# A 4-mixer decoder trunk on one core: its recorder's account learns which large buffers are free, and lane stages wait for them

## The chip, the core and the metric

The kernel runs on one core of a Trainium2 chip. The metric is the device time of one execution in microseconds (us); three runs of the kernel before gave 3057.76, 3059.04 and 3060.28 us, median 3059.04 us.

## The reference

Two layers of a trunk over 1024 prompt tokens and 8 x 8 sample tokens (1088 in all), model width 1024, in float32:

```python
for l in range(DEPTH):                       # 2 layers
    h = rmsnorm(x, norm_w[l]).astype(dt)
    proj = h @ w_in[l]                       # 1024 x 10 000 columns, in 16 parts
    ...
    y_a = a_b * conv_out * jax.nn.silu(a_z)  # A: short convolution
    y_s, h_r, h_i = s5_ssm(s_u, ...)         # B: S5, 32 groups of 16 channels, 64 complex states
    o_c, S_c = gated_recurrence(q_c, k_c, v_c, logf_c, st_hg[l])   # C: 4 heads
    o_d, S_d = gated_recurrence(q_d, k_d, v_d, gk, st_gla[l])      # D: 4 heads
    p = jnp.einsum('blnw,nwd->blnd', branches, w_branch[l])
    gates = jax.nn.sigmoid(m_logit.reshape(bsz, L, N_BRANCH, D_MODEL))
    x = x + jnp.sum(gates * p, axis=2) @ w_out[l]
```

The outputs are the normed tokens and the final states of the four mixers.

## The kernel before

All work is written from one recording program, the class `Trunk`. The large matrix products (projections, branch and output products) are its **main stream**: units of TensorE matmuls into tiles `mm`, each matmul 272 columns wide, each operand split into a high and a low part (`whi`, `wlo` for weights, `xh`/`xl`, `hi`/`lo`, `xc` for the tokens). VectorE makes each `wlo` and adds product results into half tiles `spot`; ScalarE makes each `whi`.

Beside it four **lanes** hold Python generators: `aux`, `s5l` (the S5 mixer), `tabs`, `rec` (the recurrences of C and D). After every few main matmuls `pump` looks whether a lane's next stage may be written now, and if so writes all instructions of that stage, on all engines. Engines work off their own instructions in the order written, so what `pump` decides is the order within each engine, PE's above all. `pump` decides by an **account**, the class `Book`: for every engine the time at which it will be free, and for every tile when it is written (`wr`) and last read (`rd`), from a cost for each instruction. A stage's `yield` says from which time on its next part may be written, and how many large tiles it takes (`need`).

Large tiles share 38 **places** of one pool (`NBIG`), handed round as they come free: whoever writes into a place first must wait until its last reader is done. In the account before, a new tile has no history, so its first writer counts as free to begin whenever its engine was last free.

The S5 mixer of a layer is built in **four blocks** (`s5_tables`, then `s5_scan`) while the gate products run (`GATES`), in the windows from 350 to 750 us for layer 0 and from 1840 to 2250 us for layer 1. A block's table part goes: GpSimd writes `tm` and `et` (six instructions of 128 x 512) and some 16 small ones (`qp`, `qt`); VectorE writes `tm` again from `Ppow` and `s5pk`, then `gt`, twice; TensorE turns `et` into `sm` and ScalarE copies it to `E`; GpSimd clears `tm`, VectorE copies `s5b` into it, TensorE multiplies `tm` with `s5b` and `gt`; two rounds of DMAs through `ksc` bring the result into `apad`; then TensorE multiplies `E` with `apad`, and the scan follows on VectorE. The scan of a block ends with products of `gt` and `H`, after which their places come free and the next block's `et` and `gt` take them. Ahead of block 1, VectorE prepares `s5b` through `s5tmp` from two GpSimd DMAs.

```python
            for ln in self.lanes:
                if (ln.q and ln.ready <= self.now and self.bank(ln.nsm) <= self.now and self.fits(ln)
                        and self.nc.free["dve"] <= self.now + self.backlog):
                    self.stage(ln)
```

Of the kernel before, what the change touches and what calls it, by code (L numbers as in the profile page):

```python
# [26 lines left out]
NBIG = 38  # L27
# [17 lines left out]
WBUF = 5  # L45
KEEP = 5
SPARE5 = 6
LEAD = 0.7


TURNS = (-2, 5, 11)
# [8 lines left out]
SEM = 0.05  # L60
# [36 lines left out]
class Book:  # L97
    def __init__(self, nc):
        self.nc = nc
        self.free = dict.fromkeys(("pe", "act", "dve", "pool", "sp", "dma"), 0.0)  # L100
        self.wr, self.rd = {}, {}
        self.table = None
        for attr, key in (("tensor", "pe"), ("scalar", "act"), ("vector", "dve"), ("gpsimd", "pool"), ("sync", "sp")):
            setattr(self, attr, Meter(self, getattr(nc, attr), key))

    def enter(self, key, op, aps, func):
        out, ins = aps[0], aps[1:]
        n = 1
        for d in max((x.shape[1:] for x in aps), key=lambda d: math.prod(d)):
            n *= d  # L110
        free, us = self.free, 1e-3
        parts = [self.parts_of(x) for x in aps]
        wr = [max(self.wr.get(k, 0.0) for k in p) for p in parts]
        rd = [max(self.rd.get(k, 0.0) for k in p) for p in parts]
        start = max([free[key]] + [t + SEM for t in wr[1:]])

        if key == "pe":
            start = max(start, rd[0] + SEM)
        else:
            start = max(start, rd[0] + SEM, wr[0] + SEM if op != "dma_start" else 0.0)  # L120
        if op == "dma_start":
            free[key] = start + (0.75 if key == "pool" else 0.45)
            size = math.prod(out.shape) * 4.0
            free["dma"] = max(free["dma"], free[key]) + size / 350e3
            end = free["dma"] + 1.9
        else:
            if key == "pe":
                m = math.prod(aps[-1].shape[1:]) if op == "matmul" else 128
                c = (m / 2400 + 0.011 if aps[1].dtype == F32R else 2 * max(m / 1200 + 0.004, 0.109)
                     if op == "matmul" else 0.11)  # L130
            elif key == "act":
                c = 0.155 + n * 0.87 * us
                if func in TABLED and func != self.table:
                    self.table = func
                    c += 1.3
            elif key == "dve":
                c = 0.15 + n * 1.05 * us
            else:
                c = 0.4 if n < 128 else 0.15 + n * (2.4 if op.startswith("tensor_t") or op in ("tensor_mul", "tensor_add", "tensor_sub")
                               else 0.9) * us  # L140
            free[key] = end = start + c
        for p in parts[1:]:
            for k in p:
                self.rd[k] = max(self.rd.get(k, 0.0), end)
        for k in parts[0]:
            self.wr[k] = end
# [25 lines left out]
class Trunk:  # L172
    def __init__(self, ctx, tc, a, o):
        self.tc, self.nc, self.a, self.o = tc, Book(tc.nc), a, o
        ctx.enter_context(tc.manual_schedule())
        mk = lambda name, bufs, **k: ctx.enter_context(tc.tile_pool(name=name, bufs=bufs, **k))
        self.cp = mk("const", 1)
        self.dr = mk("dram", 1, space=DRAM)
        self.ps = mk("psum", 2, space=PSUM)
        self.wp = mk("weights", 3)  # L180
        self.sp = mk("small", 1)
        self.bp = mk("big", NBIG)
        self.n = 0
        self.lanes = []
        self.banks = []
        self.alive = set()
        self.keep = KEEP
        self.backlog = BACKLOG
        self.inside = None
        self.more = False  # L190
        self.u_done = 0
        self.defer = []
# [19 lines left out]

    def free(self, *aps):
        for x in aps:
            self.alive.discard(x.name)

    def fits(self, ln):
        if ln.when and not ln.when():
# [3 lines left out]
    def pump(self):  # L222
        again = True
        while again:
            again = False
            self.weights()
            for ln in self.lanes:
                if (ln.q and ln.ready <= self.now and self.bank(ln.nsm) <= self.now and self.fits(ln)
                        and self.nc.free["dve"] <= self.now + self.backlog):
                    self.stage(ln)  # L230
                    again = True
                    break
# [33 lines left out]
    def big(self, shape, dt=F32, name="b"):  # L266
        n = 1
        for s in shape[1:]:
            n *= s
        assert n <= T, shape  # L270
        if self.inside is None:
            self.make_room()
        t = self.bp.tile([128, T], dt, tag="big", name=self.nm(name))
        v = t[:shape[0], :n]
        self.alive.add(v.name)
        assert len(self.alive) <= NBIG, sorted(self.alive)
        if len(shape) == 2:
            return v
        names = "abcdef"[: len(shape) - 1]
        return v.rearrange(f"p ({' '.join(names)}) -> p {' '.join(names)}", **dict(zip(names, shape[1:])))  # L280
# [72 lines left out]
    def parts_by(self, j):  # L353
# [38 lines left out]
                src = a22  # L392
                drop = [e + 2]

        old = self.places[-WBUF:][0] if len(self.places) >= WBUF else ()
        yield 1, max([self.at(src[:])] + [nc.rd.get(x, 0.0) + SEM for x in old])
        hi = self.wp.tile([128, 4, 128], F32R, tag="whi", name=self.nm("whi"), bufs=WBUF)
        lo = self.wp.tile([128, 4, 128], F32R, tag="wlo", name=self.nm("wlo"), bufs=WBUF)
        self.places.append((hi[:].name, lo[:].name))
        h, lv, r = hi[:], lo[:], src[:]  # L400
        if perm in (1, 2):
            h, lv = (x.rearrange("q k (p g) -> q k g p", g=8) for x in (h, lv))
# [311 lines left out]
    def make_plan(self):  # L714
        self.plan, self.seq = [], []
        self.loaded, self.done, self.raws, self.ws, self.sums_ = set(), set(), {}, {}, {}
        self.nraw = self.di = self.wi = 0
        self.preps, self.places = [], []
        self.merging = False
        self.left = [0.0] * RAWS  # L720

# [411 lines left out]
    def recurrence(self, l, nh, q, f, k, v, vs, sz, y_dst, nw_col, s0, sp_out, ss_out, gate=None):  # L1133
# [4 lines left out]
        if gate is not None:  # L1138
            yield self.at(k, *v), 1, 3
            f = yield from gate  # L1140
# [3 lines left out]
        own = self.prod([(q, k, slice(0, 128))], T, cuts, heads)  # L1144
# [13 lines left out]
            Ah = [(A[:, hh, :], hs) for hh, hs in enumerate(heads)]  # L1158
            self.free(q)
        B = k  # L1160
        yield self.at(*own[1]), 0
        own, ready = self.parts(own, cuts, heads)
        yield ready, 1, 1

# [48 lines left out]
        for _ in adv:  # L1213
            pass
        self.free(f)
        yield self.at(*pair[1]), 0
        pair, ready = self.parts(pair, cuts, heads)
        yield ready, 1
        for hh, hs in enumerate(heads):
# [117 lines left out]
        for b in range(8):  # L1337
            c = slice(TP + 8 * b, TP + 8 * b + 8)
# [30 lines left out]
        for hh in range(nh):  # L1369
# [22 lines left out]
            for c in cuts:  # L1392
                nc.vector.tensor_mul(sq[:, c], o[:, c], o[:, c])
                nc.scalar.activation(hi[:, c], o[:, c], AF.Square)
            yield self.at(hi), 0
            _, ready = self.parts((sq, (hi, lo)), cuts, heads[:1] if nh == 1 else [slice(0, 128)])
            self.alive.add(sq.name)
            yield ready, 1
            for s, n in SP:
                p = self.sm()  # L1400
# [5 lines left out]
            if len(sz) <= hh:  # L1406
                yield 0.0, 0, 0, lambda: len(sz) > hh
            nc.scalar.activation(sq, sq, AF.Exp, scale=-0.5)
            yield self.at(sq), 0
            nc.vector.tensor_mul(o, o, sq)  # L1410
            nc.vector.scalar_tensor_tensor(o, o, self.cols[:, nw_col:nw_col + 1], sz[hh], op0=ALU.mult, op1=ALU.mult)
            yield self.at(o), 0
# [6 lines left out]
    def gla_gate(self, l, pr):  # L1419
        nc = self.nc  # L1420
        f = self.big([128, T], name="f")
        m = self.big([128, T], name="m")
        bc = self.cols[:, 60 + 2 * l + pr:61 + 2 * l + pr]
        if pr == 0:
            self.r = self.big([48, T], F32R, name="r")
            for t0 in range(0, 9, 4):
                yield self.at(self.low), 1
                p = self.sm()
                n = min(512, T - 128 * t0)
                for t in range(t0, min(t0 + 4, 9)):  # L1430
                    r = 128 if t < 8 else 64
                    nc.tensor.transpose(p[:48, 128 * (t - t0):128 * (t - t0) + r], self.low[:r, t, :].bitcast(F32),
                                        self.ident[:r, :r])
                nc.scalar.activation(self.r[:, 128 * t0:128 * t0 + n], p[:48, :n], AF.Copy)
            self.free(self.low)
        yield self.at(self.r, self.wgk), 1
        for s, n in SP:
            p = self.sm()
            nc.tensor.matmul(p[:, :n], self.wgk[:, 128 * pr:128 * pr + 128], self.r[:, s:s + n], start=True, stop=True)
            nc.scalar.activation(f[:, s:s + n], p[:, :n], AF.Abs, bias=bc)  # L1440
            nc.vector.tensor_scalar(m[:, s:s + n], p[:, :n], bc, 0.0, op0=ALU.add, op1=ALU.min)
            yield 0.0, 1
        nc.scalar.activation(f, f, AF.Exp, scale=-1.0)
        nc.scalar.activation(f, f, AF.Ln, bias=self.ones[:])
        yield self.at(f), 0
        nc.vector.tensor_sub(f, m, f)
        nc.scalar.activation(f, f, AF.Exp, scale=1.0 / 16.0)
        self.free(m)
        if pr == 1:
            self.free(self.r)  # L1450
        yield self.at(f), 1, 1
        return f
# [862 lines left out]
```

## Time and profile before

| | |
|---|---|
| runs, median (lowest to highest) | 3059.04 us (3057.76 to 3060.28) |
| profiled execution: its time / span of its instructions | 3063.25 us / 3061.3 us |
| mean granted TensorE clock | 0.984 of 2.4 GHz |
| TensorE matmuls busy | 2947.9 us (96%) |
| VectorE / ScalarE / GpSimd busy | 1931.8 / 1110.3 / 389.6 us (63 / 36 / 13%) |
| share of the chain that ended last | PE 81%, DVE 7%, issue 4%, ACT 3%, DMA 2% |

PE is TensorE's matmul row, DVE is VectorE, ACT ScalarE, POOL GpSimd, SPq the queue of DMA issues. All instructions carry line 88 (89 in the changed kernel), the recorder's call, so they are told apart by tiles. The granted clock of TensorE has two levels, 0.50 (1.2 GHz) and 1.00 (2.4 GHz). Span and time of the profiled execution differ by 1.95 us, the work around the first and last instruction.

### The profile page before, as it was taken

The page shows a single profiled execution, that of the slowest core. Times are in us where ns is not written, and L with a number is a line of the kernel's source. Part 1 is how long each engine was busy: PE and PEld are TensorE (multiplying, and loading weights), DVE is VectorE, ACT ScalarE, POOL GpSimd, SP SyncE. Part 2 cuts the span into 40 slices and gives each one's busy share as a digit, 9 for nine tenths or more (in the row PEclk, how much of TensorE's full clock was granted, in tenths as well). Part 3 has the DMA queues.
Part 4 walks back from the last instruction along what each step waited for, and adds up shares of the span by engine and source line. Part 5 has one row for each costly group of instructions (what it writes and reads, how often), then busy time and mean ns, then how long its engine had stood idle before and what let it go on. Part 6 is the DMA issues. An engine that isn't in the chain of part 4 may idle for free.

```text
span 3061.3 us, 55591 instructions
## 1 busy us (share of the span) xinstructions
PE 2947.9 (96%) x22890; PEld 2862.4 (94%) x22890; DVE 1931.8 (63%) x3396; ACT 1110.3 (36%) x1932; POOL 389.6 (13%) x432
## 2 busy tenths in 40 slices
PE   7999999999999999989999999999999999999998
PEld 6999899999999999989889999999899999999997
DVE  5776676775656466868455666777645565577662
ACT  5332433333333426243343243333333344344321
POOL 2000202220000020213010002211100000103120
PEclk9999999999999999999999999999999999999999
DMA  4422333334212115435233223333421221245332
GB/s 119 162 71 61 101 111 107 106 97 143 61 47 66 40 39 183 153 102 195 88 128 107 62 72 118 100 102 110 162 63 47 63 67 37 75 160 159 133 136 89
DMA packets 318609, 309.41 MB, mean 101 GB/s; under 512 B 18497, under 2 KB 269649, under 8 KB 318357
## 3 DMA queue, kind: packets, MB, share of 16 engines
q1 hardware_dynamic: 316516, 302.02, 31.3%
q0 software_dynamic: 1840, 3.86, 0.4%
q8 instruction: 180, 2.95, 0.4%
q14 instruction: 73, 0.59, 0.1%
HBM read 217.16 MB, written 88.65 MB: 100 GB/s over the span
## 4 chain that ended last, share of the span: by engine, by line
PE 81%; DVE 7%; issue 4%; ACT 3%; DMA 2%; POOL 1%; SPq 1%; DVEq 0%; POOLq 0%; ACTq 0%
PE mm L88 70%; PE sm L88 11%; DVE wlo L88 1%; SPq L88 1%; ACT whi L88 1%; DMA apad<-usc 1%; DVE att L88 1%; DVE spot L88 1%; POOL et L88 1%; POOL tm L88 0%; DVE yb L88 0%; ACT L88 0%; DMA s5b<-in_s_b_im_dram 0%; DVE gt L88 0%; DVE wsum L88 0%
## 5 line engine op out<-in xcount | busy, mean ns | idle before, releaser
L88 PE MATMUL mm<-xc,whi 128*128 128x272 f32 x3136 | 526.7, 290 | 8.9 <-DVE spot L88 7.9
L88 PEld LDWEIGHTS mm<-xc,whi 128*128 128x128 f32 x3136 | 445.4, 191 | 12.7 <-issue 5.8
L88 DVE TENSOR_TENSOR wlo<-wraw,whi 128x512 fp32r<-128x512 f32 x400 | 315.8, 792 | 215.4 <-ACT whi L88 214.4
L88 PE MATMUL mm<-hi,whi 128*128 128x272 f32 (+2 forms) x1928 | 410.9, 293 | 12.5 <-ACT hi L88 4.3
L88 PE MATMUL mm<-lo,whi 128*128 128x272 f32 (+2 forms) x1928 | 409.5, 292 | 4.8 <-DVE lo L88 4.8
L88 PE MATMUL mm<-hi,wlo 128*128 128x272 f32 (+2 forms) x1928 | 409.2, 292 | 0.4 <-DVE wlo L88 0.4
L88 PE MATMUL mm<-xh,whi 128*128 128x272 f32 (+1 forms) x1720 | 370.5, 295 | 9.1 <-ACT spot L88 3.4
L88 PE MATMUL mm<-xl,whi 128*128 128x272 f32 (+1 forms) x1720 | 367.3, 293 | 11.7 <-DVE xl L88 11.7
L88 PE MATMUL mm<-xh,wlo 128*128 128x272 f32 (+1 forms) x1720 | 367.8, 294 | 3.4 <-DVE wlo L88 3.4
L88 ACT ACTIVATE whi<-wraw 128x512 fp32r<-128x512 f32 x400 | 272.8, 686 | 155.9 <-PE mm L88 124.2
L88 PE MATMUL mm<-xc,wlo 128*128 128x272 f32 x1568 | 326.6, 290 | 0.0
L88 PEld LDWEIGHTS mm<-hi,whi 128*128 128x128 f32 x1928 | 306.8, 191 | 15.8 <-issue 5.2
L88 PEld LDWEIGHTS mm<-lo,whi 128*128 128x128 f32 x1928 | 306.5, 191 | 7.1 <-DVE lo L88 5.8
L88 PEld LDWEIGHTS mm<-hi,wlo 128*128 128x128 f32 x1928 | 306.0, 191 | 2.6 <-issue 1.2
L88 PEld LDWEIGHTS mm<-xl,whi 128*128 128x128 f32 x1720 | 274.4, 191 | 13.4 <-DVE xl L88 12.7
L88 PEld LDWEIGHTS mm<-xh,whi 128*128 128x128 f32 x1720 | 274.3, 191 | 12.4 <-ACT whi L88 3.9
L88 PEld LDWEIGHTS mm<-xh,wlo 128*128 128x128 f32 x1720 | 273.9, 191 | 6.5 <-DVE wlo L88 5.3
L88 PEld LDWEIGHTS mm<-xc,wlo 128*128 128x128 f32 x1568 | 247.6, 190 | 0.7 <-issue 0.7
L88 ACT ACTIVATE whi<-wsum 128x512 fp32r<-128x512 f32 x147 | 99.4, 677 | 205.3 <-DVE wsum L88 172.1
L88 DVE TENSOR_TENSOR spot<-spot,mm 128x544 f32<-128x544 f32 x181 | 129.6, 716 | 53.3 <-PE mm L88 50.7
L88 ACT ACTIVATE spot<-spot 128x544 f32<-128x544 f32 x87 | 57.4, 660 | 266.2 <-DVE spot L88 264.6
L88 DVE TENSOR_TENSOR wlo<-wsum,whi 128x512 fp32r<-128x512 f32 x147 | 114.1, 776 | 54.5 <-ACT whi L88 53.3
(367 smaller groups left out, 5162.9 us busy)
## 6 DMA issues: line engine op xcount, KB each, us to landing
wraw<-in_w_in_dram SPq DMA_DIRECT2D x328, 256.0 KB
g<-gsc SPq DMA_DIRECT2D x64, 544.0 KB
gsc<-spot SPq DMA_DIRECT2D x116, 272.0 KB
y<-ysc SPq DMA_DIRECT2D x24, 544.0 KB
wraw<-in_w_branch_dram SPq DMA_DIRECT2D x48, 256.0 KB
ysc<-o SPq DMA_DIRECT2D x16, 544.0 KB
wo<-in_w_out_dram SPq DMA_DIRECT2D x16, 512.0 KB
out_dram<-S SPq DMA_DIRECT2D x12, 512.0 KB
```

Of the source, the lines that this page charges most:

```text
L88: r = fn(*a, **kw)
```

## The change

Four things change in the recorder, none in the arithmetic. (1) The account keeps for each large tile the place that it takes: `gone` lists the tiles given back, the least recently used one is taken as predecessor, and the new tile inherits the time at which that one was last used. (2) `pump` writes a lane's stage only when the `need` places that it will take are free by the account (`places`). (3) Costs: a small GpSimd instruction 0.55 instead of 0.4, a DMA with rows under 64 elements eight times its bytes. (4) Five yields in the recurrences and the gate of D, reached 30 times a layer, become due 1.0 earlier (`AHEAD`): the VectorE instructions behind them are written before ScalarE, by the account, is done. `self.places` of the weights is only renamed `pairs_`.

```diff
+AHEAD = 1.0
...
+        self.turn += 1
+        for x in aps:
+            self.used[x.name] = self.turn
...
-            size = math.prod(out.shape) * 4.0
+            size = math.prod(out.shape) * 4.0 * (8 if out.shape[-1] < 64 else 1)
...
-                c = 0.4 if n < 128 else 0.15 + n * (2.4 if op.startswith("tensor_t") or op in ("tensor_mul", "tensor_add", "tensor_sub")
+                c = 0.55 if n < 128 else 0.15 + n * (2.4 if op.startswith("tensor_t") or op in ("tensor_mul", "tensor_add", "tensor_sub")
...
-            self.alive.discard(x.name)
+            if x.name in self.alive:
+                self.alive.discard(x.name)
+                self.gone.append(x.name)
+
+    def left_at(self, x):
+
+        return max(d.get(k, 0.0) for d in (self.nc.rd, self.nc.wr) for k in (x, x + "b")) + SEM
+
+    def places(self, n):
+
+        if not n:
+            return 0.0
+        return max([self.left_at(x) for x in sorted(self.gone, key=lambda x: self.nc.used.get(x, 0))[:n]])
...
+                        and self.places(ln.need) <= self.now
...
+        old = min(self.gone, key=lambda x: self.nc.used.get(x, 0))
+        self.gone.remove(old)
+        self.nc.rd[v.name] = self.nc.rd[v.name + "b"] = self.left_at(old)
+        self.nc.used[v.name] = self.nc.turn
...
-        yield self.at(*own[1]), 0
+        yield self.at(*own[1]) - AHEAD, 0
...
-            yield self.at(sq), 0
+            yield self.at(sq) - AHEAD, 0
```

Up to the start of S5 in layer 0 nothing moves. From there, in three places:

VectorE, layer 0, the start of block 2's tables, before: `tm_5291` and `gt_5290` are block 2's; the `fs` and `s5pk` rows are the last of block 1's scan.

```order
L88 TENSOR_TENSOR s5pk_3869<-fs_5222,f_617_5223 128x4x8 x2
L88 TENSOR_TENSOR spot_3390<-spot_3853,mm_5130 128x544
L88 TENSOR_TENSOR wlo_5212<-wsum_5143,whi_5211 128x512
L88 TENSOR_TENSOR wraw_5071<-wraw_4864,wraw_5071 128x512
L88 TENSOR_TENSOR wlo_5271<-wraw_5071,whi_5270 128x512
L88 TENSOR_TENSOR tm_5291<-Ppow,s5pk_3869 128x512 x2
L88 TENSOR_TENSOR gt_5290<-tm_5291 64x4x128 x2
L88 TENSOR_TENSOR wsum_5144<-wraw_5105,wsum_5144 128x512
```

The same place now (`tm_5366`, `gt_5365`):

```order
L89 TENSOR_TENSOR s5pk_3892<-fs_5320,f_626_5321 128x4x8 x2
L89 TENSOR_TENSOR wlo_5400<-wraw_5116,whi_5399 128x512
L89 TENSOR_TENSOR spot_3853<-spot_1560,mm_5333 128x544
L89 TENSOR_TENSOR wsum_5443<-wraw_5314,wraw_5395 128x512
L89 TENSOR_TENSOR wsum_5444<-wsum_5443,wraw_5116 128x512
L89 TENSOR_TENSOR spot_3853<-spot_3853,mm_5418 128x544
L89 TENSOR_TENSOR spot_3852<-spot_1560,mm_5333 128x544
L89 TENSOR_TENSOR wlo_5453<-wsum_5444,whi_5452 128x512
L89 TENSOR_TENSOR wlo_5466<-wraw_5397,whi_5465 128x512
L89 TENSOR_TENSOR wlo_5498<-wsum_5443,whi_5497 128x512
L89 TENSOR_TENSOR tm_5366<-Ppow,s5pk_3892 128x512 x2
```

Nine rows of the main stream now stand ahead of the first `tm` where four stood. On TensorE, from block 1's last `gt` row to block 2's first `tm` row, the order holds 186 main matmuls where it held 76; between GpSimd's `et` and VectorE's `tm` pass 66 to 86 main matmuls in every block of either layer (before: 74 in the first block, none in the other three). The last block's last rows stand 337 main matmuls later in layer 0 and 241 later in layer 1; the first products of layer 0's first recurrence 34 later, those of layer 1 at the old place, and the last recurrence ends at its old place in both layers.

VectorE, layer 0, ahead of block 1, before: the `s5tmp` and `s5b` rows read what the two GpSimd DMAs bring.

```order
L88 TENSOR_TENSOR s5tmp_3870<-s5b_3868,zfac 128x256 x2
L88 TENSOR_TENSOR s5b_3868<-s5tmp_3870 128x256
L88 TENSOR_TENSOR s5tmp_3870<-s5b_3868,zfac 128x256 x2
L88 TENSOR_TENSOR s5b_3868<-s5tmp_3870 128x256
L88 TENSOR_TENSOR wlo_4009<-wraw_3745,whi_4008 128x512
L88 TENSOR_TENSOR spot_1560<-spot_3852,mm_3987 128x544
```

And now:

```order
L89 TENSOR_TENSOR wsum_4039<-wsum_4038,wraw_3745 128x512
L89 TENSOR_TENSOR spot_1560<-spot_1560,mm_4009 128x544
L89 TENSOR_TENSOR s5tmp_3893<-s5b_3891,zfac 128x256 x2
L89 TENSOR_TENSOR s5b_3891<-s5tmp_3893 128x256
L89 TENSOR_TENSOR wlo_4056<-wsum_4039,whi_4055 128x512
L89 TENSOR_TENSOR wlo_4073<-wraw_3988,whi_4072 128x512
L89 TENSOR_TENSOR spot_3390<-spot_3852,mm_3975 128x544
L89 TENSOR_TENSOR s5tmp_3893<-s5b_3891,zfac 128x256 x2
```

The first of these rows now stands 54 main matmuls later, behind two more `spot` rows; the DMAs themselves are written 18 main matmuls later.

VectorE, layer 0, start of the merge, before: `y` is mixer A's output, split for the first branch products; the `o` rows close a recurrence.

```order
L88 TENSOR_TENSOR wlo_12642<-wraw_12302,whi_12641 128x512
L88 TENSOR_TENSOR lo_12697<-y_12615,hi_12696 128x1088
L88 TENSOR_TENSOR wlo_12701<-wraw_12424,whi_12700 128x512
L88 TENSOR_TENSOR o_12536<-o_12536,osq_12558 128x1088
L88 SCALAR_TENSOR_TENSOR o_12536<-o_12536,cols,sz_11530 128x1088
L88 TENSOR_TENSOR lo_12721<-y_12617,hi_12720 128x1088
```

And now:

```order
L89 TENSOR_TENSOR o_12529<-o_12529,osq_12550 128x1088
L89 SCALAR_TENSOR_TENSOR o_12529<-o_12529,cols,sz_11527 128x1088
L89 TENSOR_TENSOR wlo_12643<-wraw_12383,whi_12642 128x512
L89 TENSOR_TENSOR lo_12699<-y_12615,hi_12698 128x1088
L89 TENSOR_TENSOR wlo_12703<-wraw_12428,whi_12702 128x512
L89 TENSOR_TENSOR lo_12719<-y_12617,hi_12718 128x1088
```

The pair of `o` rows moved from between the first two `lo` rows to ahead of the `wlo` row before them. Ahead of mixer B's products (`xl`) another such pair of `o` rows moves 22 main matmuls earlier.

## Rows read from the trace of the kernel before

**Rows 1.** The page, busy time of each engine: us, share, instructions.

```profile
PE 2947.9 (96%) x22890; PEld 2862.4 (94%) x22890; DVE 1931.8 (63%) x3396; ACT 1110.3 (36%) x1932; POOL 389.6 (13%) x432
```

**Rows 2.** Busy time by windows: length, PE, PEld, DVE, ACT, POOL (instructions), PE clock, DMA.

```profile
250.00:300.00 50.00, 50.00 (x404) 50.00 (x403) 35.02 (x52) 15.29 (x24) 0.80 (x2) 1.00 0.25 69
...
450.00:500.00 50.00, 45.89 (x375) 45.26 (x374) 32.41 (x56) 15.32 (x29) 18.25 (x25) 0.93 0.32 96
```

**Rows 3.** Waits of PE: tile, who ended it: us in total, times, longest.

```profile
PE sm L88 <- DVE tm L88: 16.8, 4, 4.4
PE mm L88 <- DVE spot L88: 14.3, 6, 3.9
PE mm L88 <- DVE xl L88: 11.7, 4, 3.7
PE sm L88 <- ACT E L88: 6.4, 2, 3.2
...
PE sm L88 <- DMA apad<-usc: 5.3, 5, 1.9
...
PE mm L88 <- DVE lo L88: 4.8, 2, 2.4
...
PE sm L88 <- POOL et L88: 3.1, 2, 1.6
```

**Rows 4.** Timeline of DVE, layer 0, tables of block 2: start, us, [idle before].

```profile
479.33 1.29 DVE L88 TENSOR_TENSOR tm<-Ppow,s5pk 128x512 f32<-128x512 f32 x2 [5.46 <-POOL et L88]
...
484.78 0.71 DVE L88 TENSOR_TENSOR spot<-spot,mm 128x544 f32<-128x544 f32 x1
...
488.15 0.82 DVE L88 COPY tm<-s5b 64x64 f32<-64x64 f32 x4
```

**Rows 5.** Timeline of POOL, the same block.

```profile
474.48 1.29 POOL L88 TENSOR_TENSOR et<-tm 128x512 f32<-128x512 f32 x1 [5.35 <-issue]
...
478.01 1.29 POOL L88 TENSOR_TENSOR et<-tm 128x512 f32<-128x512 f32 x1
479.24 0.83 POOL L88 COPY qp<-Qpow 128x4 f32<-128x4 f32 x2
...
487.57 0.40 POOL L88 MEMSET tm<- 128x368 f32 x1
```

**Rows 6.** Timeline of PE, layer 0, waits at block 2 and at block 3.

```profile
488.69 0.62 PE L88 MATMUL sm<-s5b,tm 128*32 128x16 f32 x4 [4.04 <-DVE tm L88]
...
578.27 0.77 PE L88 MATMUL mm<-xc,whi 128*128 128x272 f32 x4 [2.37 <-DVE spot L88]
```

**Rows 7.** Timeline of DVE, layer 0, ahead of block 1.

```profile
365.14 0.42 DVE L88 TENSOR_TENSOR s5tmp<-s5b,zfac 128x256 f32<-128x256 f32 x1 [3.67 <-DMA s5b<-in_s_b_im_dram]
...
369.68 0.68 DVE L88 TENSOR_TENSOR wsum<-wraw,wraw 128x512 f32<-128x512 f32 x1
370.40 1.67 DVE L88 TENSOR_TENSOR wsum<-wsum,wraw 128x512 f32<-128x512 f32 x1
```

**Rows 8.** Timeline of POOL, the same stretch.

```profile
369.73 1.79 POOL L88 TENSOR_TENSOR et<-tm 128x512 f32<-128x512 f32 x1
```

**Rows 9.** Windows as in rows 2, the nine stretches of S5 at clock 0.50, and their sum.

```profile
1996.17:1999.58 3.41, 3.41 (x29) 2.91 (x26) 0.29 (x1) 1.54 (x4) 0.00 (x0) 0.50 0.50 151
...
sum 51.21, PE 42.22 PEld 39.47 DVE 29.69 ACT 16.96 POOL 9.22; mean PE 4.69 PEld 4.39 DVE 3.30 ACT 1.88 POOL 1.02
```

**Rows 10.** Windows as in rows 2, stretches of the merge at clock 0.50.

```profile
1183.80:1187.21 3.41, 3.41 (x16) 3.26 (x15) 3.02 (x5) 1.27 (x3) 0.00 (x0) 0.50 0.29 81
...
2695.90:2699.32 3.42, 3.42 (x16) 3.40 (x16) 3.04 (x5) 1.53 (x3) 0.00 (x0) 0.50 0.34 92
```

**Rows 11.** Timeline of DVE, layer 0, start of the merge.

```profile
1176.84 1.29 DVE L88 TENSOR_TENSOR lo<-y,hi 128x1088 fp32r<-128x1088 f32 x1 [4.67 <-ACT hi L88]
...
1178.65 1.29 DVE L88 TENSOR_TENSOR o<-o,osq 128x1088 f32<-128x1088 f32 x1
...
1181.24 3.69 DVE L88 TENSOR_TENSOR lo<-y,hi 128x1088 fp32r<-128x1088 f32 x3
```

More of the change, by code (lines that the diff above doesn't have):

```diff
@@ L101, in __init__ @@
         self.wr, self.rd = {}, {}
+        self.turn, self.used = 0, {}
         self.table = None
@@ L186, in __init__ @@
         self.alive = set()
+        self.gone = [f"none{i}" for i in range(NBIG)]
         self.keep = KEEP
@@ L393, in parts_by @@
                 drop = [e + 2]
-        old = self.places[-WBUF:][0] if len(self.places) >= WBUF else ()
+        old = self.pairs_[-WBUF:][0] if len(self.pairs_) >= WBUF else ()
         yield 1, max([self.at(src[:])] + [nc.rd.get(x, 0.0) + SEM for x in old])
@@ L398, in parts_by @@
         lo = self.wp.tile([128, 4, 128], F32R, tag="wlo", name=self.nm("wlo"), bufs=WBUF)
-        self.places.append((hi[:].name, lo[:].name))
+        self.pairs_.append((hi[:].name, lo[:].name))
         h, lv, r = hi[:], lo[:], src[:]
@@ L717, in make_plan @@
         self.nraw = self.di = self.wi = 0
-        self.preps, self.places = [], []
+        self.preps, self.pairs_ = [], []
         self.merging = False
@@ L1215, in recurrence @@
         self.free(f)
-        yield self.at(*pair[1]), 0
+        yield self.at(*pair[1]) - AHEAD, 0
         pair, ready = self.parts(pair, cuts, heads)
@@ L1394, in recurrence @@
                 nc.scalar.activation(hi[:, c], o[:, c], AF.Square)
-            yield self.at(hi), 0
+            yield self.at(hi) - AHEAD, 0
             _, ready = self.parts((sq, (hi, lo)), cuts, heads[:1] if nh == 1 else [slice(0, 128)])
             self.alive.add(sq.name)
+            self.gone.remove(sq.name)
             yield ready, 1
@@ L1444, in gla_gate @@
         nc.scalar.activation(f, f, AF.Ln, bias=self.ones[:])
-        yield self.at(f), 0
+        yield self.at(f) - AHEAD, 0
         nc.vector.tensor_sub(f, m, f)
```

## The prediction

> **What bounds the kernel now.** The page first: TensorE's matmuls are busy 2947.9 us, 96% of the span, VectorE only 63% [rows 1]. So the kernel is bound by TensorE, and a change that leaves every matmul as it is can win only what TensorE idles (3061.3 - 2947.9 = 113 us) and what it loses at the lower clock. The windows say where. In a stretch with no S5 work TensorE is busy 50.00 of 50 us and gets through 404 matmuls, 0.124 us each; in a stretch in which S5 tables are built it is busy 45.89, gets through 375, and its mean clock is 0.93 [rows 2]. The list of TensorE's waits then says for whom [rows 3]. Three entries are S5 tables alone: VectorE's `tm` 16.8 us in 4 waits, ScalarE's `E` 6.4 in 2, GpSimd's `et` 3.1 in 2. Of the six waits for `spot` (14.3 us) one stands at block 3, 2.37 us long [rows 6], with a twin in layer 1. Tables therefore cost 16.8 + 6.4 + 3.1 + 4.7 = 31.0 us, and the other four `spot` waits, 9.6 us, stand ahead of block 1.
>
> The timelines of one block show why. GpSimd's first `et` can begin only when block 1's last product with `gt` has freed its place: 474.48, after idling [rows 5]. The second ends at 479.30, and until then VectorE stands 5.46 us at `tm` [rows 4], with `wlo` and `spot` rows of the main stream written behind it: the `spot` row comes at 484.78. GpSimd goes on with 16 small instructions and clears `tm` only at 487.57 to 487.97; VectorE's copy follows at 488.15, and TensorE, which had got there long before, goes on at 488.69 after 4.04 us [rows 6]. The cause is the order: VectorE's `tm` was written at the very point of the main stream at which the places came free, since the account let GpSimd begin in the past.
>
> **What the clock adds.** Nine stretches of S5 show a granted clock of 0.50, the level of 1.2 GHz; each but one begins in or right behind one of these waits. TensorE is busy 42.22 us in them [rows 9]. Leaving out the one that begins at 1996.17 (3.41 us, behind a DMA), 38.8 us at half speed lose at most 19.4 us.
>
> **The change, part by part.** It adds and removes no arithmetic; what counts is where rows stand.
>
> *Tables.* From `et` to VectorE's `tm` now lie 66 to 86 main matmuls, 8.2 to 10.7 us, and the trace needs 479.33 - 474.48 = 4.85 us [rows 4, 5]: no wait, with 3.3 us to spare. From the freed place to the end of the clearing it needs 487.97 - 474.48 = 13.5 us; TensorE's `tm` row now stands 186 main matmuls (23 us) behind, where it stood 76 (9.4 us). All 31.0 us should go. Bounds: 0 and -31.0.
>
> *Ahead of block 1.* VectorE stood 3.67 us at `s5tmp` for a DMA [rows 7], with `spot` behind it. These rows now stand 54 main matmuls (6.7 us) later, the DMAs 18 (2.2 us) later: 4.5 us gained. That covers layer 0; layer 1, where the longest `spot` wait was 3.9 us [rows 3], I leave 1.6 us. So -8.0 of 9.6; bounds 0 and -9.6.
>
> *Clock.* With the waits gone most of the 19.4 us comes back. Part of these stretches is many small S5 matmuls that stay, so I take -15; bounds 0 and -19.4.
>
> *What is late next.* Behind the `tm` product comes the way through two DMAs to `apad`, and there TensorE already waits 5.3 us in five of eight blocks [rows 3]. The slow stretches lie just in this way and gave the DMAs time; of the 15 us some will be waited for here. I take +5; bounds 0 and +15.
>
> *GpSimd beside VectorE.* In blocks 2 to 4 VectorE stood idle while GpSimd wrote `tm` and `et`; now it does main work there. Ahead of block 1 this can be seen: a `wsum` row takes 1.67 us instead of 0.68 [rows 7] beside an `et` of 1.79 us [rows 8], which takes 1.29 alone [rows 5]. Six such GpSimd instructions a block can each hold one VectorE row: at most 6 x 0.99 = 5.9 us. VectorE is busy 35.02 of 50 us without S5 [rows 2], so 8.5 us hold 2.5 us of slack. With half of the meetings, 3.0 - 2.5 = 0.5 us a block stays, 4 us in eight; bounds 0 and 8 x 3.4 = 27. I take +4, since the two `wsum` rows side by side show one hit and one not.
>
> The Trainium skill speaks against this change here: the page SBUF — State Buffer, section "Who interferes with whom", says that a VectorE instruction with two SBUF inputs contends with a GpSimd instruction that reads SBUF, and that the later one is fully blocked until the first is finished. The stretched row agrees, being 0.99 us longer where an `et` alone takes 1.29. By the rule all six would block for 1.29 us, 7.7 - 2.5 = 5.2 us a block, 42 us instead of 4.
>
> *Merge.* The `o` pair (1181.24 - 1178.65 = 2.6 us) moves ahead of the first `lo`, into time in which VectorE idled 4.67 us [rows 11], so the two waits for `lo`, 4.8 us [rows 3], should go: -4.8, bounds 0 and -4.8. The waits for `xl` (11.7 us in 4) lose such a pair out of a full VectorE queue too: up to 2.6 us a layer, of which I take 2: -4, bounds 0 and -11.7. The slow stretches behind the `lo` waits [rows 10] are worth 6.83 / 2 = 3.4 us at most: -2.
>
> *`AHEAD`, costs, renaming: nothing.* VectorE may stand up to 1.0 us at 60 places for ScalarE. What hides it: a stand of 5.46 us cost TensorE 4.04 [rows 4, 6] and one of 4.67 us cost 2.4 [rows 11, 3], so the first 1.4 us or more are covered by finished weights and free PSUM. Without cover it is 60 x 1.0 us; bounds 0 and +60, and I take the lower end, since 1.0 is under both covers. SP's queue keeps its issues, some of them moved.
>
> **The sum.** -31.0 - 8.0 - 15 + 5 + 4 - 4.8 - 4 - 2 = -55.8 us. The profiled execution took 3063.25 us, 4.2 above the median of the runs; off that it is 3007.5, off the median 3003.2. I predict 3003.
>
> **The rivals.**
> - *GpSimd now slows VectorE.* For it: the stretched row. Against: VectorE's 30% idle. At the upper bound 27 us instead of 4, and the clock falls again in eight blocks, up to half of the 15 us given back: 3003 + 23 + 7.5 = 3034; it reaches from 3022 to 3046. By the page's rule in place of the row it would be 3003 + 38 = 3041 before the clock.
> - *Nothing moves.* The account's guess of the place could be wrong, and the waits only change their names: 3059. Against: the distances in the order hold whatever place is taken.
> - *Slower: the last block comes too late.* It ends 337 and 241 main matmuls later, 42 and 30 us, among the recurrences, which `begin(3)` drains before the last branch. If the delay came through to there in full, TensorE would idle 72 us: 3075. It makes the kernel slower when over 62 us of the 72 (the gain and 6 us) arrive. Against: by the order the last recurrence ends at its old place in both layers.
> - *All terms at their best:* -31.0 - 9.6 - 19.4 - 4.8 - 11.7 - 3.4 = -79.9, so 2979.
>
> **How the numbers follow.** Forecast (2985 to 3022) 0.62; GpSimd slows VectorE (3022 to 3046) 0.18; nothing moves 0.06; slower 0.06; better than 2985 0.08. The range 2985 to 3046 holds the first two, 0.80; the forecast's own is 2985 to 3022. A change of under 0.2% (6 us) can't be told from none in this kernel. Faster: 0.62 + 0.18 + 0.08 = 0.88. Of "nothing moves" 0.04 falls within 6 us and 0.02 beyond; slower 0.06 + 0.02 = 0.08.
>
> **What the changed kernel's profile would show.** Tables: TensorE's waits for `tm`, `E` and `et` gone, VectorE's for `et` too. Head: no `s5tmp` wait of over 1.5 us for the DMA. Clock: mean of 0.988 or more, and fewer than five stretches at 0.50 in S5. `apad` waits 5 to 15 us. Merge: no `lo` wait. I am wrong if `spot` or `wlo` waits appear beside GpSimd's tables, if `apad` takes over what the tables give back, or if TensorE idles before the last branch.

## The result, and the profile after

The changed kernel took 2993.86 us (median of four runs, 2990.29 to 2994.76) beside 3059.66 us for the kernel before: ratio 0.9781, 95% interval 0.9764 to 0.9798, 66 us faster. The forecast was 3003, in a range of 2985 to 3046. Its profiled execution spans 2992.0 us at a mean clock of 0.992, 69.3 us less than before.

The page of the changed kernel, busy time of each engine (answers to [rows 1]):

```profile
PE 2926.8 (98%) x22890; PEld 2845.6 (95%) x22890; DVE 1944.8 (65%) x3396; ACT 1111.8 (37%) x1932; POOL 382.1 (13%) x432
```

TensorE idles 2992.0 - 2926.8 = 65.2 us where it idled 113.4, so 48.2 us of the gain are waits. The other 21.1 us are TensorE's own busy time, for the same 22890 matmuls: that is clock. The windows show both in one row, the window from 450 to 500 us as in the second of [rows 2], and behind it the only stretch of S5 that is left at 0.50:

```profile
450.00:500.00 50.00, 50.00 (x430) 49.85 (x428) 35.56 (x59) 17.78 (x31) 15.56 (x25) 1.00 0.39 120
...
668.27:671.69 3.42, 3.38 (x15) 3.38 (x16) 0.00 (x0) 1.31 (x3) 1.26 (x7) 0.50 0.22 81
```

TensorE's waits in the changed kernel (answers to [rows 3]):

```profile
PE mm L89 <- DVE xl L89: 10.7, 4, 3.2
...
PE mm L89 <- ACT hi L89: 4.5, 2, 2.5
...
PE sm L89 <- DMA apad<-usc: 3.2, 7, 0.7
PE sm L89 <- ACT ys L89: 3.1, 2, 2.1
...
PE mm L89 <- DVE lo L89: 0.5, 2, 0.2
```

VectorE's `tm` and `spot`, ScalarE's `E` and GpSimd's `et` are no longer in the list. `xl` has hardly moved, `apad` fell, and `ys` is new.

VectorE in block 2 of layer 0 (answers to [rows 4]):

```profile
485.60 0.69 DVE L89 TENSOR_TENSOR wlo<-wsum,whi 128x512 fp32r<-128x512 f32 x1
486.21 1.28 DVE L89 TENSOR_TENSOR tm<-Ppow,s5pk 128x512 f32<-128x512 f32 x2
```

GpSimd there (answers to [rows 5]):

```profile
475.20 1.29 POOL L89 TENSOR_TENSOR et<-tm 128x512 f32<-128x512 f32 x1 [2.67 <-issue]
...
479.06 1.29 POOL L89 TENSOR_TENSOR et<-tm 128x512 f32<-128x512 f32 x1
...
496.09 0.41 POOL L89 MEMSET tm<- 128x368 f32 x1 [10.49 <-DVE gt L89]
```

The second `et` ends at 480.35 and `tm` begins at 486.21, straight behind a `wlo` row and with no wait in brackets: 5.9 us to spare. GpSimd still idles ahead of `et`; only nobody stands behind it now.

### The profile page after: what moved, and what is told of

Its sections match the earlier page's. It is cut to its first block, busy times and chain, and to the rows that moved or that the text cites. A ratio compares the mean times of both kernels' runs of the same rounds, so it can differ in the third digit from the quotient of the medians.

```text
span 2992.0 us, 55595 instructions
## 1 busy us (share of the span) xinstructions
PE 2926.8 (98%) x22890; PEld 2845.6 (95%) x22890; DVE 1944.8 (65%) x3396; ACT 1111.8 (37%) x1932; POOL 382.1 (13%) x432
## 4 chain that ended last, share of the span: by engine, by line
PE 86%; DVE 6%; DMA 3%; ACT 2%; issue 2%; SPq 1%; POOL 0%; DVEq 0%; POOLq 0%; ACTq 0%
PE mm L89 75%; PE sm L89 12%; SPq L89 1%; DMA apad<-usc 1%; DVE wlo L89 1%; DVE att L89 1%; DMA wraw<-in_w_branch_dram 1%; DVE yb L89 0%; ACT whi L89 0%; DVE mg L89 0%; DVE g L89 0%; DMA sz<-szs 0%; DVE o L89 0%; DVE xl L89 0%; DVE xf L89 0%
## 5 line engine op out<-in xcount | busy, mean ns | idle before, releaser
L89 PE MATMUL mm<-xc,whi 128*128 128x272 f32 x3136 | 519.4, 288 | 1.0 <-ACT xc L89 0.8
L89 PEld LDWEIGHTS mm<-xc,whi 128*128 128x128 f32 x3136 | 439.2, 188 | 2.4 <-ACT xc L89 1.0
L89 DVE TENSOR_TENSOR wlo<-wsum,whi 128x512 fp32r<-128x512 f32 x147 | 120.2, 818 | 55.2 <-ACT whi L89 53.2
```

The lines of the kernel that those rows point to most:

```text
L89: r = fn(*a, **kw)
```

## The experiments

Ratios are to the kernel before, measured beside each run; differences are ratio times 3060 us, since medians of different groups of runs differ by some 3 us.

| kernel | median us | ratio, 95% interval | us against before |
|---|---|---|---|
| changed kernel | 2993.9 | 0.9781 (0.9764 to 0.9798) | -67.0 |
| parts 1 and 2 | 3013.8 | 0.9843 (0.9829 to 0.9858) | -48.0 |
| part 1 | 3013.8 | 0.9842 (0.9829 to 0.9856) | -48.3 |
| clamp instead of part 1 | 3013.0 | 0.9846 (0.9832 to 0.9859) | -47.1 |
| all but the inheritance | 3038.8 | 0.9928 (0.9915 to 0.9940) | -22.0 |
| part 3 | 3049.8 | 0.9958 (0.9944 to 0.9971) | -12.9 |
| all but the DMA cost | 3003.8 | 0.9815 (0.9802 to 0.9829) | -56.6 |
| part 4 | 3046.9 | 0.9949 (0.9937 to 0.9962) | -15.6 |
| all but AHEAD | 3000.2 | 0.9805 (0.9792 to 0.9819) | -59.7 |
| changed, `et` twice | 2998.7 | 0.9789 (0.9772 to 0.9806) | -64.6 |
| changed, tables on VectorE | 2990.2 | 0.9765 (0.9749 to 0.9781) | -71.9 |
| changed, YLAG 1 | 2987.1 | 0.9749 (0.9734 to 0.9764) | -76.8 |
| the same, products with sz last | 2986.9 | 0.9751 (0.9736 to 0.9767) | -76.2 |

**Parts 1 and 2, and part 1 alone.** From the changed kernel:

```diff
-AHEAD = 1.0
+AHEAD = 0.0
-            size = math.prod(out.shape) * 4.0 * (8 if out.shape[-1] < 64 else 1)
+            size = math.prod(out.shape) * 4.0
-                c = 0.55 if n < 128 else ...
+                c = 0.4 if n < 128 else ...
```

and for part 1 alone also

```diff
-                        and self.places(ln.need) <= self.now
```

> The changed kernel with the old costs and AHEAD = 0, so parts 1 and 2 (places in the account, lane wait) alone. VectorE's tm stands 70 to 76 main matmuls behind GpSimd's et in every block, and the rows ahead of block 1 only 24 main matmuls (3.0 us) later than before, the two DMAs likewise not moved away from them. Theory A (the order of et and tm behind the freed place makes the gain): TensorE's waits for tm, E and et and VectorE's for et gone, 31.0 us, and 15 to 19 us of clock; the spot waits ahead of block 1 (9.6 us) stay; 3059.7 - 31.0 - 17 = 3012, within 3002 to 3020. Theory B (costs and AHEAD carry a large part of the 65.8 us): 3030 or more. GpSimd beside VectorE costs 0 to 4 us.

> As the run before, but also without the condition that a lane stage waits for its places, so part 1 alone. By the order GpSimd's tables come 2 main matmuls earlier and all later S5 rows stand where they stood. Theory A1 (what counts is the inherited time in the account, which puts VectorE's tm behind et; the lane wait does nothing beyond that): the same time as the run before within 3 us. Theory A2 (the lane wait makes part of the gain): 10 us or more slower than the run before.

Both took 48 us off, as theory A and A1 had it. TensorE's waits with parts 1 and 2:

```profile
PE mm L89 <- DVE spot L89: 8.7, 2, 4.7
...
PE sm L89 <- DMA apad<-usc: 5.5, 5, 2.4
...
PE mm L89 <- DVE lo L89: 5.1, 3, 2.4
```

The tables' waits are gone, and the two `spot` waits left stand ahead of block 1. TensorE's busy time is 2930.5 us of a span of 3013.0: 17.4 us less busy (clock) and 30.9 us less idle than before. The lane wait, the second of the four edits, did nothing that can be measured beside part 1 (48.0 with it, 48.3 without, each known to some 4 us).

**A clamp in place of the account of places.** From the kernel before, one line in `s5_tables` ahead of GpSimd's six instructions:

```diff
+        nc.free["pool"] = max(nc.free["pool"], self.now)
```

> The kernel before with one line ahead of GpSimd's tables: the account may not let GpSimd begin earlier than the present point of the main stream. No places, no lane wait, old costs, AHEAD absent. By the order VectorE's tm stands 70 main matmuls behind et in blocks 2 to 4, the rows ahead of block 1 do not move. Theory A (only the distance between et and tm counts, however the account comes to it): the tables' waits go as with parts 1 and 2, 48 us less than before, within 42 to 53. Rival (it matters that the account knows which place is taken): at most half of that, 24 us less or fewer.

47.1 us. So which place is taken does not matter here; that GpSimd may not begin in the account's past does.

**All but the inheritance.** From the changed kernel:

```diff
-        self.nc.rd[v.name] = self.nc.rd[v.name + "b"] = self.left_at(old)
```

> The changed kernel without the one line by which a new large tile inherits the time at which its place was last used; the bookkeeping of places, the lane wait, costs and AHEAD stay. Theory A (that line carries the tables' gain): VectorE's tm stands at GpSimd's et again in blocks 2 to 4, the waits for tm, E, et and spot there come back, and what is left is what costs and AHEAD gave, 28 us less than before: 3030, within 3024 to 3042. Rival (the lane wait does the work): 2994 to 3005.

The gain fell from 67 to 22 us, and TensorE's list has the tables again, now as one wait in each of blocks 2 to 4 of either layer:

```profile
PE mm L89 <- DVE spot L89: 21.6, 4, 5.7
PE sm L89 <- DVE tm L89: 14.6, 2, 7.3
```

The six waits, four for `spot` and two for `tm`, make 36.2 us where the tables' waits were 31.0; `E` and `et`, which were expected back, are not among them. Taken away alone the line costs 45 us and given alone it brings 48.

**Part 3, and all but the DMA cost.** Part 3 in the kernel before, and the changed kernel without the factor of eight:

```diff
-            size = math.prod(out.shape) * 4.0
+            size = math.prod(out.shape) * 4.0 * (8 if out.shape[-1] < 64 else 1)
-                c = 0.4 if n < 128 else ...
+                c = 0.55 if n < 128 else ...
```

```diff
-            size = math.prod(out.shape) * 4.0 * (8 if out.shape[-1] < 64 else 1)
+            size = math.prod(out.shape) * 4.0
```

> The kernel before with the two new costs (0.55 for a small GpSimd instruction, eight times the bytes of a DMA with short rows), so part 3 alone. The rows ahead of block 1 stand where the changed kernel has them; in blocks 2 to 4 VectorE's tm still stands at the very point of GpSimd's et. Theory A: the s5tmp wait for the DMA and the spot waits ahead of block 1 (9.6 us) go, with up to 3 us of clock; the waits for tm, E and et (about 31 us) stay: 3046 to 3053. Theory B (the costs make a large part of the gain): 3030 or less. It also prices apad: the time by which TensorE waits for apad tells whether those waits depend on the head.

> The changed kernel without the eightfold bytes of DMAs with short rows; the cost 0.55, AHEAD, places and lane wait stay. By the order the rows ahead of block 1 stand where the kernel with parts 1 and 2 alone had them. Theory A (that cost made the gain of the head): the s5tmp wait for the DMA and two spot waits of 3.9 and 4.7 us come back, 9 to 13 us above the changed kernel's 2994: 3003 to 3007. Rival (the head is covered by the other parts too): 2994 to 2998.

12.9 us gained and 10.4 us lost: both times are as theory A had them. TensorE's waits with part 3 alone:

```profile
PE mm L88 <- DVE spot L88: 21.5, 4, 5.7
PE sm L88 <- DVE tm L88: 14.6, 2, 7.3
...
PE sm L88 <- DMA apad<-usc: 3.4, 2, 2.2
```

and with all but the DMA cost:

```profile
PE mm L89 <- DVE spot L89: 7.1, 2, 4.0
...
PE sm L89 <- DMA apad<-usc: 5.5, 5, 2.1
```

The waits ahead of block 1 go with part 3 and two of them are back without the DMA cost, so the head's rows follow the account's cost of one kind of DMA. The tables' waits did not stay as they were, though: with part 3 alone `E` and `et` are gone from the list and the six `spot` and `tm` waits, one in each of blocks 2 to 4, make 36.1 us in place of 31.0. The `apad` waits are lower with this cost in both pairs: 3.4 us beside 5.3 before, and 3.2 in the changed kernel beside 5.5.

**Part 4, and all but part 4.** The kernel before with `AHEAD = 1.0` at the five yields, and the changed kernel with:

```diff
-AHEAD = 1.0
+AHEAD = 0.0
```

> The kernel before with AHEAD = 1.0 at the five yields, so part 4 alone. No S5 row moves. Theory A: tables and clock in S5 stay as they are; only rows of the recurrences and the merge move, so the lo waits (4.8 us) and part of the xl waits (11.7 us) may go: 3050 to 3060, and all S5 waits as before. Theory B: 3040 or less. Third possibility: VectorE stands at 60 places for ScalarE and it is slower than 3062.

> The changed kernel with AHEAD = 0; by the order no S5 row moves. Alone the five yields took 15.6 us off the kernel before. Theory C (in the changed kernel part of that was already there or is lost, since the parts sum to 79 us and together give 66): 6 to 10 us above the changed kernel, 3000 to 3004, with lo waits and two hi waits in the merge back. Rival (the parts add up and the loss is elsewhere): 14 to 18 us above, 3008 to 3012.

Alone it brought 15.6 us, more than theory A's 0 to 10 and short of theory B's 20; inside the changed kernel it is worth 7.3 us, as theory C had it. Waits of TensorE with part 4 alone:

```profile
PE sm L89 <- DVE tm L89: 16.9, 4, 4.4
...
PE mm L89 <- DVE xl L89: 10.6, 4, 4.3
...
PE mm L89 <- ACT hi L89: 1.0, 2, 0.5
...
PE mm L89 <- DVE lo L89: 0.5, 2, 0.2
```

The S5 waits stay, as expected. But besides `lo` the two `hi` waits went (4.3 us before), and in the changed kernel they are still there, 4.5 us. That is part of why the parts alone sum to 48.3 + 12.9 + 15.6 = 76.8 us and together give 67.0, a difference that is little more than the intervals allow (each figure is known to 4 or 5 us). Which of the merge's rows keeps `hi` late was not taken apart.

**GpSimd beside VectorE: more of it, and none.** The changed kernel with `et` written twice, and with the tables' six instructions on VectorE:

```diff
         e.tensor_sub(et[:, 0], tm[:, 0], tm[:, 1])
+        e.eng.tensor_sub(et[:, 0], tm[:, 0], tm[:, 1])
...
         e.tensor_add(et[:, 1], tm[:, 0], tm[:, 1])
+        e.eng.tensor_add(et[:, 1], tm[:, 0], tm[:, 1])
```

```diff
-        e = nc.gpsimd
+        e = nc.vector
         e.tensor_mul(tm[:, 0], P[0], Bv[0])
...
+        e = nc.gpsimd
         for i in range(2):
             e.tensor_copy(qp[:, 0, i], self.Q[:, i, lj, 8])
```

> The changed kernel with each of GpSimd's two et instructions of a block written twice, the second time past the account, so no row moves: 16 more GpSimd instructions of 1.27 to 1.8 us, and et later by 2.6 to 3.6 us a block. VectorE's tm stands 5.8 us behind the end of the second et in block 2 of the changed kernel's trace (486.2 against 480.4), so it should not wait. Theory D (a GpSimd instruction beside VectorE stretches a VectorE row by at most 1 us, and VectorE's idle time covers it): within 4 us of the changed kernel, 2990 to 2998, TensorE's ys waits up to 2 us longer each. Rival (VectorE is held in full and TensorE sees it): 16 x 1.3 = 21 us or more above it, 3010 or more.

> The changed kernel with the six 128 x 512 instructions of a block's tables on VectorE in place of GpSimd: no GpSimd instruction of that size is left beside the end of the scan. 48 instructions of 0.69 us, 33 us, more on VectorE, 61 us less on GpSimd; VectorE's busy share goes from 65 to 66%. Theory D (the two ys waits, 3.1 us, and their slow stretch come from rows of VectorE stretched beside these tables): the ys waits go, 2 to 5 us below the changed kernel, 2988 to 2992, if the added VectorE work is covered. Rival (33 us more on VectorE hold up main rows beside the tables): spot or wlo waits there and 3000 or more.

With `et` twice, the page:

```profile
PE 2927.0 (98%) x22890; PEld 2845.0 (95%) x22890; DVE 1953.2 (65%) x3396; ACT 1108.7 (37%) x1932; POOL 411.2 (14%) x448
```

VectorE is busy 1953.2 - 1944.8 = 8.4 us longer for 16 more GpSimd instructions, 0.53 us for each, while TensorE's busy time stands still; the time is 2.4 us above the changed kernel, inside the intervals. The `ys` waits did not grow (3.0 us); two small entries are new in TensorE's list, `spot` with 1.0 and `E` with 0.9 us. With the tables on VectorE, the page:

```profile
PE 2924.6 (98%) x22890; PEld 2843.3 (95%) x22890; DVE 1951.9 (65%) x3444; ACT 1109.8 (37%) x1932; POOL 320.1 (11%) x384
```

The same six instructions there (VectorE's timeline, block 4 of layer 0):

```profile
653.88 1.41 DVE L89 TENSOR_TENSOR H<-w 64x512 f32<-64x512 f32 x2
...
656.70 1.28 DVE L89 TENSOR_TENSOR tm<-Ppow,s5b 128x512 f32<-128x512 f32 x2
658.01 0.69 DVE L89 TENSOR_TENSOR et<-tm 128x512 f32<-128x512 f32 x1
658.74 1.29 DVE L89 TENSOR_TENSOR tm<-Ppow,s5b 128x512 f32<-128x512 f32 x2
660.07 0.69 DVE L89 TENSOR_TENSOR et<-tm 128x512 f32<-128x512 f32 x1
```

They add 1.28 + 0.69 + 1.29 + 0.69 = 3.95 us a block, 31.6 us in eight, yet VectorE is busy only 7.1 us longer: its other rows are 24.5 us shorter, 0.51 us for each of the 48 GpSimd instructions that are gone. The `ys` wait is no longer in TensorE's list. The median is 4.9 us under the changed kernel's by ratio, but the intervals overlap; that the `ys` wait came from GpSimd is shown, that this version is faster is not.

**`xl`: written earlier.** The changed kernel with

```diff
-YLAG = 3
+YLAG = 1
```

and, on top of it, the products of `yv` and `sz` in steps of their own behind the last `xl`:

```diff
             nc.vector.tensor_sub(lo, t, hi.bitcast(F32))
+
+        def gate(j):
+            t = self.su[j]
             nc.vector.tensor_mul(t, t, sz[j])
             self.free(sz[j])
...
+        self.defer += [lambda j=j: gate(j) for j in range(4)]
```

> The changed kernel with YLAG = 1 for 3: the steps that split mixer B's output into xh and xl are written two steps of the main stream earlier. Nothing before the merge moves. Theory E (the four xl waits, 10.7 us, are rows of VectorE written too late, beside a recurrence's osq, sql and o): most of them go and with them up to three half-clock stretches of 3.4 us, 8 to 15 us below the changed kernel: 2979 to 2986. Rival (the data come late: yv from its DMA or ScalarE's xh): the waits stay under another name, within 3 us of 2994.

> As the run before, and the four products of yv with sz (1.29 us each on VectorE), which stood between the xl rows, are written after the last of them. Theory E: whatever xl wait is left goes too, 0 to 4 us below the run before, 2976 to 2985. Rival: the products are then late for the yb rows that read them, and yb or hi waits come up: 2 to 6 us above the run before.

The first is 9.8 us under the changed kernel by ratio, the second 9.2; the intervals just touch. TensorE's waits with YLAG 1:

```profile
PE sm L89 <- DVE sql L89: 8.2, 4, 3.3
...
PE mm L89 <- DVE xl L89: 1.7, 2, 0.9
PE mm L89 <- ACT xh L89: 1.7, 2, 0.9
...
PE mm L89 <- ACT hi L89: 1.0, 2, 0.5
```

`xl` fell by 9.0 us and `hi` by 3.5, so these rows were late mostly by their place, not for their data; 1.7 us came back under the name of ScalarE's `xh`, which the rival had named. Against the gain stands `sql`, 8.2 us: the recurrence whose rows `xl` has overtaken is now late itself. The profiled execution spans 2987.7 us, only 4.3 less, so the size of this gain is less sure than its sign. With the `sz` products last, `sql` is 4.3 and `xl` 6.2, 10.5 us where the two were 9.9: `xl` rose, against theory E, and no `yb` or `hi` wait came up, against the rival. By their medians these two are the fastest kernels of this study; with the tables on VectorE as well it was not tried.

## Why the prediction was right, and where its terms were off

The mechanism held: the account let GpSimd begin in the past, so VectorE's `tm` was written at the very point of `et`. Parts 1 and 2 bring 48 us, the sum put 31.0 + 15 on tables and clock; without the one line of inheritance the wait is back; and a clamp that knows nothing of places brings the same. None of the signs named for being wrong came up; of what the profile was to show, the `apad` waits (5 to 15 us) came out otherwise, and of `lo` 0.5 us is left. Term by term, from the waits and windows of the two profiled executions:

| term | predicted | measured | |
|---|---|---|---|
| tables | -31.0 | -31.0 | all four entries gone |
| ahead of block 1 | -8.0 | -9.6 | both layers, not layer 0 alone |
| clock in S5 | -15 | -19.4 | (42.22 - 3.38) / 2 |
| `apad` | +5 | -2.1 | wrong sign |
| GpSimd beside VectorE | +4 | +3.1 | at `ys`, not at the tables |
| `lo` | -4.8 | -4.3 | |
| `xl` | -4 | -1.0 | |
| clock in the merge | -2 | -1.4 | TensorE busy 29.6, now 26.7 us at 0.50 behind S5 |

The measured terms make -65.7 of the 69.3 us; the two clock rows, 20.8 us, agree with the 21.1 us by which TensorE's busy time fell. The forecast of -55.8 was 10 us short, above all at `apad` (7.1) and the clock in S5 (4.4); `xl` went 3.0 the other way.

**Clock.** The 4.4 us kept back for small S5 matmuls had no ground: with the waits gone these run at the full clock too, and the stretch behind the DMA at 1996.17 [rows 9] went with them.

**`apad`, the step that failed.** I took the way through the DMAs as a fixed time, so that a faster TensorE would have to wait for it. The queue shows otherwise. Before, block 2 of layer 0:

```profile
497.08 0.34 SPq L88 DMA_DIRECT2D gsc<-spot  x1
497.52 4.67 SPq L88 DMA_DIRECT2D apad<-ksc  x8
```

and in the changed kernel:

```profile
505.18 0.34 SPq L89 DMA_DIRECT2D gsc<-spot  x1
505.62 3.71 SPq L89 DMA_DIRECT2D apad<-ksc  x8
```

Ahead of the `apad` issues stands a `gsc` issue, and it goes out when ScalarE's `spot` of the main stream is done:

```profile
504.49 0.66 ACT L89 ACTIVATE spot<-spot 128x544 f32<-128x544 f32 x1 [0.98 <-DVE spot L89]
```

504.49 + 0.66 = 505.15, and the issue follows at 505.18. TensorE's `tm` product there:

```profile
499.09 0.30 PE L89 MATMUL sm<-s5b,tm 128*32 128x16 f32 x4
```

So the way hangs on the main stream itself: from the `tm` product to this issue it took 497.08 - 488.69 = 8.4 us [rows 6], most of them at the lower clock (487.48 to 494.31), and takes 505.18 - 499.09 = 6.1 now. In this block it sped up with the clock that was to outrun it: with 104 main matmuls between the `tm` product and the product with `apad` in both kernels, the wait fell from 1.27 to 0.25 us.

That is not the whole of it. In block 3, where no `gsc` issue stood in between before and one does now, the way to the first `apad` issue grew from 4.4 to 4.8 us in layer 0, and waits of 0.46 and 0.66 us are new in the two layers. And the clock alone did not lower the `apad` waits: with parts 1 and 2, which bring most of the clock back, they stand at 5.5 us, 0.2 above before, and at 5.5 too in the changed kernel without the DMA cost; in these two kernels 92 main matmuls stand in block 2 between the two products, and TensorE waits 1.45 to 2.41 us. With the clamp, which has neither the DMA cost nor the places, they are 2.7 us. So the +5 came in none of these kernels, and the waits change with where the order puts the product with `apad`; how each part moves it was not taken apart.

**GpSimd beside VectorE.** The estimate, half of 6 x 0.99 us a block, was 0.5 us for each GpSimd instruction, and the two experiments give 0.53 and 0.51; VectorE's idle time covers it at the tables, as forecast. What was missed is that block 4's tables of layer 0 now run beside the end of block 3's scan. GpSimd there:

```profile
658.75 2.08 POOL L89 TENSOR_TENSOR tm<-Ppow,s5b 128x512 f32<-128x512 f32 x2
660.91 1.62 POOL L89 TENSOR_TENSOR et<-tm 128x512 f32<-128x512 f32 x1
```

VectorE:

```profile
659.01 0.72 DVE L89 TENSOR_TENSOR spot<-spot,mm 128x544 f32<-128x544 f32 x1 [0.40 <-PE mm L89]
659.77 3.32 DVE L89 TENSOR_TENSOR H<-w 64x512 f32<-64x512 f32 x2
663.12 0.97 DVE L89 TENSOR_TENSOR fs<-s5pk,Qpow 128x64 f32<-128x64 f32 x1
...
666.47 0.71 DVE L89 TENSOR_TENSOR spot<-spot,mm 128x544 f32<-128x544 f32 x1
```

Two `H` rows take 3.32 us where they take 1.41 with the tables on VectorE. The rows behind them are stretched too or late (`fs` takes 0.97 us, there 0.23), the `spot` row among them; ScalarE stands for that `spot` with the `ys` copy written behind it:

```profile
667.21 0.66 ACT L89 ACTIVATE spot<-spot 128x544 f32<-128x544 f32 x1 [10.04 <-DVE spot L89]
667.78 0.88 ACT L89 COPY ys<-sm 128x408 f32<-128x408 f32 x2
```

and TensorE waits 2.06 us for `ys`:

```profile
668.31 0.82 PE L89 MATMUL sm<-apad 128*128 128x136 f32 x2 [2.06 <-ACT ys L89]
```

The one stretch of S5 at 0.50 begins here, at 668.27. The second `ys` wait, 1.04 us in layer 1, was not followed row by row.

The Trainium skill, page SBUF — State Buffer, section "Who interferes with whom", has it that a VectorE instruction with two SBUF inputs contends with a GpSimd instruction that reads SBUF, and that one with at most one SBUF input, outside the 2-port modes, does not. The trace agrees: `H`, with both inputs in SBUF, is stretched, and `spot`, which reads `mm` from PSUM, takes 0.72 us beside the same GpSimd row. The 42 us that I worked out by the rule did not come: a GpSimd instruction cost VectorE 0.5 us in the mean and not 1.29. That a row often meets only what is left of a GpSimd instruction, or none, would explain this; it was not shown row by row.

**`xl`.** The wait was put down to a pair of `o` rows in VectorE's queue; with these moved it lost 1.0 us. Writing the `xl` rows themselves earlier took 9.0.

Of the rivals, "nothing moves" and "the last block comes too late" left no sign: TensorE's idle time from the end of S5 to the end of the layer, the recurrences and the last branch included, fell from 15.1 to 12.9 us in layer 0 and from 22.7 to 18.5 us in layer 1.

## What to carry to other kernels

Where a planner writes the order, look for resources that it holds to be free at once: each engine that may "begin in the past" puts another engine's row, and all rows queued behind it, in front of a wait. A floor at the present point was worth as much here as exact bookkeeping. A way through DMAs need not be a fixed time: where its issue stands in a queue behind a row of the stream that it is measured against, as in block 2 here, the two speed up together. Read what stands ahead of it in the queue before a faster engine is charged for it.

## What the runs showed that I had not expected

A GpSimd instruction of 128 x 512 beside VectorE cost VectorE 0.53 us when 16 were added and 0.51 us when 48 were taken away, so by one profile each the price is nearly the same from either side. And parts that each gain alone, 48.3, 12.9 and 15.6 us, gave 9.8 us less together; 8.3 of that stand at part 4, worth 15.6 us alone and 7.3 in the changed kernel.
